# Attention output with plain fp32 values, two tiles side by side in the column halves of the matrix array

## The chip, the cores and the metric

The kernel runs on one core of a Trainium2 chip. The metric is device time in microseconds (us) for one launch; lower is better. The core has five engines that run their own instruction streams and wait for each other through semaphores: TensorE (PE; its weight loads are listed apart as PEld), VectorE (DVE), ScalarE (ACT), GpSimd (POOL) and SyncE (SP, which here only issues DMAs). Matrix products read SBUF and write PSUM; the other engines bring results from PSUM back to SBUF.

## The reference, cut to what matters

One mixer layer over 2048 latent tokens (a grid of 32 rows by 64 columns) and 256 context tokens, width 1024: RMSNorm with modulation, one input projection, two groups of heads, one output projection, gated residual, final RMSNorm. The group that the change touches is neighbourhood attention with 8 heads of 64:

```python
s_loc = einsum('bhrqd,bhrkd->bhrqk', qr, kg) * scale + bias      # window of 8 x 16 cells
s_ctx = einsum('bhrqd,bhcd->bhrqc', qr, k_ctx) * scale           # all 256 context keys
p = softmax(concatenate([where(mask, s_loc, -inf), s_ctx], -1))
o = einsum('bhrqk,bhrkd->bhrqd', p_loc, vg) + einsum('bhrqc,bhcd->bhrqd', p_ctx, v_ctx)
y_na = merge(o) * silu(na_g)
```

The other group is retention (a chunkwise recurrence). Everything is float32.

## The kernel before, in words

**Precision.** Most products are made from operands that are split into a rounded part (fp32r) and its remainder; three of the four cross products are summed in PSUM. A few products, the retention's and the modulation's (`ada_mm`, L296), use plain fp32 operands; each such matmul is recorded as two weight loads and two matmuls, one pass after the other.

**Stages.** First the projections (L343, L354, L656), whose results go to DRAM scratch tensors. The values are made by `u_v`: ACT copies the projected tile as rounded part, DVE subtracts for the remainder, and both 64-column pieces are stored side by side as 128 columns per head in `vB` (latent) and `vS` (context). The attention stage follows, then retention and the output projection.

**The attention stage.** A head's 2048 queries are cut into 16 tiles of 128 queries (8 rows by 16 columns, `dims`): index i over row bands, j over column bands. With 8 heads there are 128 tiles, and one step of the main loop (`for t in range(NT + 3)`) works on four of them at once, in a software pipeline written out by hand:

- `s_mm(t)`: scores of tile t into the PSUM tile `sS` (L1019, local keys and context keys, two halves of the split query each);
- `s_norm(t - 1)`: DVE reciprocal (L1038), POOL multiplies the probabilities (L1039);
- `s_min(t)`: DVE adds the bias and takes the row's maximum (L1028);
- `p_tr(t - 2)`: PE transposes 3 or 4 local groups of keys (L1046) and 2 context groups (L1048) into the PSUM tile `tr`; ACT copies them to `pt` as the rounded part (L1050);
- `s_exp(t)`: ACT exponential (L1033);
- `p_lo(t - 2)`: DVE subtracts the rounded part from `tr` for the remainder (L1056);
- `pv(t - 3)`: PE multiplies values by probabilities. The stationary operand holds 128 columns (rounded value, remainder), the moving one 256 (rounded probability, remainder), so that one matmul makes four partial products (L1067 local, L1069 context);
- every second step `combine`: ACT copies one partial product (L1090), DVE adds three of them (L1091, L1093), and for every fourth tile POOL multiplies by the gate (L1097).

Between these, `fill` issues pieces of the remaining projections, about two a step: six matmuls of 256 columns (L354) or three of 512 (L343). When such a unit ends, its own DVE, ACT or POOL work is issued at that place: for the rotary q projection three DVE operations (L382, L383, L384), for the rotary k projection four (L418, L419). All engines take their instructions in the written order. `load_v`, `load_gate`, `load_q` and `bias` issue their DMAs on SP, stores go through ACT's queue.

Of the kernel before, what the change touches and what calls it, by code (L numbers as in the profile page):

```python
# [18 lines left out]
P = 128  # L19
# [61 lines left out]
def hybrid_kernel(ctx: ExitStack, tc: tile.TileContext, a: dict, out: bass.AP):  # L81
# [5 lines left out]
    kS = [dram.tile([P, 2, LT], F32, name=f"kS{t}") for t in range(4)]  # L87
    vS = [dram.tile([LC, 4, P], F32, name=f"vS{t}") for t in range(2)]
    vB = [dram.tile([P, 8, 4, 4 * P], F32, name=f"vB{t}") for t in range(2)]
    gS = [dram.tile([P, L], F32, name=f"gS{t}") for t in range(4)]  # L90
# [297 lines left out]
    def u_v(w, c0, tp):  # L388
        pm = yield from tokform(w, tp)
        vt = op.tile([P, 4, 4, 64], F32R, name="o")  # L390
        pv = pm.rearrange("p (g e d) -> p g e d", e=2, d=64)
        nc.scalar.copy(vt[:, :, ::3, :], pv)
        nc.vector.tensor_tensor(vt[:, :, 1:3, :], pv, f(vt)[:, :, ::3, :], ALU.subtract)
        s, o = (c0 - 1024) // WG, f(vt).rearrange("p (t h) e d -> p t (h e d)", t=2)
# [584 lines left out]
    def load_head(h):  # L979
        k2 = kp.tile([P, LT], F32R, name="k2")  # L980
        for hl in range(2):
            nc.sync.dma_start(f(k2)[64 * hl:64 * hl + 64, :], kS[h // 2][64 * (h % 2):64 * (h % 2) + 64, hl, :])
        vc = kp.tile([P, 2, P], F32R, name="vc")
        nc.sync.dma_start(f(vc), vS[h // 4][:, h % 4, :].rearrange("(n p) d -> p n d", p=P))
        return dict(k2=k2, h=h, vc=vc, vt={}, q={})
# [8 lines left out]
    def load_v(hd, gs):  # L994
        for g in gs:
            vt, h = kp.tile([P, 4, P], F32R, name="vt", bufs=6), hd["h"]
            for e, n in ((0, P), (2, 96)):
                nc.sync.dma_start(f(vt)[:n, e:e + 2, :], vB[h // 4][:n, g, e:e + 2, (h % 4) * P:(h % 4 + 1) * P])
            hd["vt"][g] = vt
# [4 lines left out]

    heads, ys, tl_st = {}, {}, {}

# [34 lines left out]
    def p_tr(t):  # L1041
# [8 lines left out]
        nc.scalar.copy(pt[:, :ng_ + 2, 0, :], tr[:, :ng_ + 2, :])  # L1050
        T.update(pt=pt, ng=ng_)

    def p_lo(t):
        T = tl_st[t]
        pt, n = T["pt"], T["ng"] + 2
        nc.vector.tensor_tensor(pt[:, :n, 1, :], tr[:, :n, :], f(pt)[:, :n, 0, :], ALU.subtract)  # L1056

    def pv(t):
        h, i, j, kr0, kr, kc0, cw = dims(t)
        T, hd = tl_st[t], heads[h]  # L1060
        pt, ng_ = T["pt"], T["ng"]
        if t % 2 == 0:
            tl_st["po"] = psc.tile([P, 2, 2, P], F32, name="po")
        po = tl_st["po"]
        cn = 4 * cw
        for g in range(ng_):
            nc.tensor.matmul(po[:, t % 2, :, :], hd["vt"][kr0 // 4 + g][:cn, VORD.index(j), :], pt[:cn, g, :, :], start=(g == 0), stop=False)  # L1067
        for g in range(2):
            nc.tensor.matmul(po[:, t % 2, :, :], hd["vc"][:, g, :], pt[:, ng_ + g, :, :], start=False, stop=(g == 1))  # L1069
        del tl_st[t]  # L1070

# [5 lines left out]
    def load_gate(t):  # L1077
        h, i = dims(t)[:2]
        gts[t // 4] = ap_.tile([P, 512], F32, name="gt", bufs=2)
        nc.sync.dma_start(gts[t // 4][fin_(h)], gS[h // 2][fin_(h), i * 512:(i + 1) * 512])  # L1080

    def combine(t):
        h, i, j = dims(t)[:3]
        po, jp = tl_st["po"], j // 2
        fin, oth = fin_(h), fin_(h + 1)
        if jp == 0:
            ys[i] = ap_.tile([P, 512], F32, name="y2", bufs=2)
        y2 = ys[i]
        tmp = ap_.tile([P, 2, P], F32, name="cmb", bufs=1)
        nc.scalar.copy(tmp[fin], po[oth, :, 0, :])  # L1090
        nc.vector.tensor_tensor(tmp[fin], po[fin, :, 0, :], tmp[fin], ALU.add)  # L1091
        yv = y2[fin].rearrange("p (r w c) -> p w r c", r=8, w=4)[:, 2 * jp:2 * jp + 2]
        nc.vector.tensor_tensor(yv, po[fin, :, 1, :].rearrange("p j (r c) -> p j r c", r=8),  # L1093
                                tmp[fin].rearrange("p j (r c) -> p j r c", r=8), ALU.add)
        if jp == 1:
            gt = gts.pop(t // 4)
            nc.gpsimd.tensor_tensor(y2[fin], y2[fin], gt[fin], ALU.mult)  # L1097
            store(yS[i // 2][h // 2, fin, (i % 2) * 512:(i % 2) * 512 + 512], y2[fin], 2)

# [125 lines left out]
    for t in range(NT + 3):  # L1225
# [392 lines left out]
```

## Time and profile before

| | |
|---|---|
| time, median of 3 runs | 1346.33 us (1343.83 to 1348.54) |
| the profiled execution, its own time | 1343.91 us |
| its span in the trace | 1342.1 us |
| busy: PE, PEld, DVE, ACT, POOL | 96%, 86%, 62%, 45%, 43% |
| granted TensorE clock | 0.996 |

The span is what the trace covers of that execution; 1.8 us lie around it. Matmuls are pipelined: a row's duration includes the way through the array, so the time that a matmul costs in a stream is read from the distance between two starts. In rows of the timeline the first number is the start, the second the time until the last one of the row ends; "x4" counts the instructions in it. In a group's row stand busy time and the mean of one in ns, and behind the bar how long its engine stood idle just before, and what it waited for. `128*32` means 128 rows and 32 columns of the array.

### The profile page before, as it was taken

What the parts mean: (1) busy time and instruction counts of PE and PEld (TensorE: products, weight loads), DVE (VectorE), ACT (ScalarE), POOL (GpSimd) and SP (SyncE); (2) the same over time, 40 slices, a digit from 0 to 9 for tenths busy, and PEclk for the clock granted to TensorE, in tenths of its full rate; (3) what the DMA queues carried; (4) which work ended last, traced back from release to release, by engine and by line L of the source; (5) the groups of instructions that cost most, each with busy time, mean ns of one, the idle gap of its engine ahead of it and who ended that gap; (6) DMA issues with size and microseconds to landing.
All of it is one profiled execution on the core that took longest, in us unless ns stands there. A gap on an engine that the chain in (4) does not pass through costs nothing. (4 is left out here: it accounts for less than half of the span.)

```text
span 1342.1 us, 23118 instructions
## 1 busy us (share of the span) xinstructions
PE 1292.9 (96%) x8252; PEld 1148.2 (86%) x8252; DVE 831.2 (62%) x1442; ACT 602.5 (45%) x1252; POOL 574.9 (43%) x567
## 2 busy tenths in 40 slices
PE   5989999999999999999999999999999999999997
PEld 2677899887898889998999889889999788888886
DVE  4786365876676763477767777776654734444445
ACT  3454334243434334555565466556643244333432
POOL 3452102455115664454535365655523154544442
PEclk9999999999999999999999999999999999999999
DMA  9386797565867657967587887776547888445433
GB/s 362 142 282 235 267 321 207 188 219 185 320 181 230 217 176 244 256 205 196 155 219 211 231 221 210 188 183 197 157 158 255 283 288 269 156 157 173 165 128 123
DMA packets 172084, 287.24 MB, mean 214 GB/s; under 512 B 17345, under 2 KB 92225, under 8 KB 170690
## 3 DMA queue, kind: packets, MB, share of 16 engines
q1 hardware_dynamic: 139554, 228.35, 56.5%
q10 hardware_dynamic: 32416, 57.42, 11.9%
q8 instruction: 66, 1.08, 0.4%
q14 instruction: 48, 0.39, 0.1%
HBM read 194.48 MB, written 91.23 MB: 213 GB/s over the span
## 5 line engine op out<-in xcount | busy, mean ns | idle before, releaser
L354 PE MATMUL mm<-whi,hlo 128*128 128x256 f32 x832 | 228.1, 282 | 1.0 <-DMA hlo<-cS 1.0
L354 PE MATMUL mm<-whi,hhi 128*128 128x256 f32 x768 | 224.3, 292 | 0.0
L354 PE MATMUL mm<-wlo,hhi 128*128 128x256 f32 x768 | 216.8, 282 | 0.0
L1050 ACT CAST pt<-tr 128x640 fp32r<-128x640 f32 (+1 forms) x128 | 95.5, 746 | 160.3 <-PE tr L1048 157.7
L1056 DVE TENSOR_TENSOR pt<-tr,pt 128x640 fp32r<-128x640 f32 (+1 forms) x128 | 113.9, 890 | 78.3 <-ACT pt L1050 77.1
L354 PEld LDWEIGHTS mm<-whi,hlo 128*128 128x128 f32 x832 | 155.9, 190 | 1.4 <-DMA hlo<-cS 1.3
L1039 POOL TENSOR_SCALAR sp<-sp,stt 128x640 f32<-128x640 f32 (+2 forms) x128 | 103.2, 808 | 106.5 <-DVE stt L1038 77.8
L354 PEld LDWEIGHTS mm<-whi,hhi 128*128 128x128 f32 x768 | 146.1, 190 | 0.0
L354 PEld LDWEIGHTS mm<-wlo,hhi 128*128 128x128 f32 x768 | 145.7, 190 | 0.0
L610 POOL TENSOR_TENSOR whi<-st,whi 128x512 fp32r<-128x512 f32 x48 | 64.7, 1370 | 158.7 <-ACT whi L609 158.7
L1028 DVE CUSTOM_DVE_ANT_0 sp<-sS,nb 128x640 f32<-128x640 f32 (+2 forms) x128 | 105.6, 825 | 34.1 <-DMA nb<-in_rpb_t_dram 21.5
L1033 ACT ACTIVATE sp<-sp,stt 128x640 f32<-128x640 f32 (+2 forms) x128 | 107.4, 839 | 20.5 <-DVE stt L1028 19.3
L343 PE MATMUL mm<-hhi,whi 128*128 128x512 f32 x256 | 108.6, 424 | 0.5 <-ACT hhi L261 0.5
L343 PE MATMUL mm<-hlo,whi 128*128 128x512 f32 x256 | 102.0, 398 | 5.8 <-DVE hlo L282 2.4
L1019 PE MATMUL sS<-k,q 128*128 128x256 f32 (+3 forms) x512 | 99.1, 315 | 5.7 <-DVE stt L1028 5.5
L343 PE MATMUL mm<-hhi,wlo 128*128 128x512 f32 x256 | 101.7, 397 | 0.0
L1459 PE MATMUL mm<-wor,y 128*128 128x512 f32 x384 | 95.6, 398 | 1.7 <-DVE xt L1468 1.2
L656 PE MATMUL mm<-hhi,whi 128*128 128x512 f32 x336 | 96.8, 393 | 0.0
L1468 DVE TENSOR_TENSOR xt<-mm,xt 128x512 f32<-128x512 f32 x64 | 43.9, 687 | 82.5 <-PE mm L1459 82.5
L1019 PEld LDWEIGHTS sS<-k,q 128*128 128x128 f32 x512 | 82.7, 188 | 12.6 <-DVE stt L1028 8.8
L1459 PE MATMUL mm<-won,y 128*128 128x512 f32 x336 | 89.1, 403 | 0.0
L1459 PEld LDWEIGHTS mm<-wor,y 128*128 128x128 f32 x384 | 69.9, 188 | 18.0 <-issue 3.7
(253 smaller groups left out, 3018.3 us busy)
## 6 DMA issues: line engine op xcount, KB each, us to landing
st<-in_w_in_dram SPq DMA_DIRECT2D x64, 512.0 KB
q<-qS SPq DMA_DIRECT2D x64, 256.0 KB
hlo<-hS SPq DMA_DIRECT2D x20, 512.0 KB
k<-kS SPq DMA_DIRECT2D x16, 576.0 KB
kS<-o SPq DMA_DIRECT2D x16, 512.0 KB
vB<-o SPq DMA_DIRECT2D x64, 128.0 KB
qS<-o ACTq DMA_DIRECT2D x16, 512.0 KB
woS<-g ACTq DMA_DIRECT2D x32, 256.0 KB
```

The lines of the kernel that those rows point to most:

```text
L343: nc.tensor.matmul(pm[:, :n], ww[:, k, cs], h[:, k, :], start=(k == 0 and i == 0), stop=(k == KC - 1 and i == 2))
L354: nc.tensor.matmul(pm[:, t * WG:(t + 1) * WG], h[:, k, o:o + P], ww[:, k, :], start=(k == 0 and i == 0), stop=(k == KC - 1 and i == 2))
L610: nc.gpsimd.tensor_tensor(t[:, 1], r, f(t)[:, 0], ALU.subtract)
L656: nc.tensor.matmul(pm, ww[:, k, :], hh[:, k, :], start=(k == 0 and i == 0), stop=(k == KH - 1 and i == 2))
L1019: nc.tensor.matmul(o, hd["q"][i][:, hl, j * P:(j + 1) * P], k, start=(hl == 0), stop=(hl == 1))
L1028: nc.vector.tensor_tensor_reduce(T["sp"][:, :n], T["s"], nbz[big][:, o:o + n], -1.0, 3e38, ALU.add, ALU.min, T["st"][:, 0:1])
L1033: nc.scalar.activation(sp[:, :n], sp[:, :n], AF.Exp, bias=st[:, 0:1], scale=-1.0, accum_out=st[:, 1:2])
L1039: nc.gpsimd.tensor_scalar(sp[:, :n], sp[:, :n], st[:, 2:3], 0.0, ALU.mult, ALU.add)
L1050: nc.scalar.copy(pt[:, :ng_ + 2, 0, :], tr[:, :ng_ + 2, :])
L1056: nc.vector.tensor_tensor(pt[:, :n, 1, :], tr[:, :n, :], f(pt)[:, :n, 0, :], ALU.subtract)
L1459: nc.tensor.matmul(pm, yy[:, k, :], ww[:, k, sl], start=(k == 0 and i == 0), stop=(k == 3 and i == 2))
L1468: nc.vector.tensor_tensor(xts[t][:, sl], pm, xts[t][:, sl], ALU.add)
```

## The change

Values and probabilities stay plain fp32 in the product of scores and values. `u_v` only copies (ACT); a head's values have 64 columns in `vB`, `vS`, `vt` and `vc`. `p_lo` goes: ACT copies the local groups of `tr` to `pt`, and DVE (`p_ctx`, new) copies the two context groups. `pv` now takes two tiles, j and j + 1 of one row band: tile j's result goes to PSUM partitions 0 to 63, that of j + 1 to partitions 64 to 127, with a stationary operand of 64 columns and 128 moving columns, and the two tiles' matmuls alternate. `pv` is called in every second step. `combine` is called in every fourth step, and is two DVE multiplies of PSUM by the gate; ACT's copy, DVE's two additions and POOL's multiply go. The gate is loaded into both halves of the partitions, by two DMAs instead of one. `po` is half as large and allocated once for four tiles; `pt` is half as large and has four buffers instead of two.

```diff
     def u_v(w, c0, tp):
         pm = yield from tokform(w, tp)
-        vt = op.tile([P, 4, 4, 64], F32R, name="o")
-        pv = pm.rearrange("p (g e d) -> p g e d", e=2, d=64)
-        nc.scalar.copy(vt[:, :, ::3, :], pv)
-        nc.vector.tensor_tensor(vt[:, :, 1:3, :], pv, f(vt)[:, :, ::3, :], ALU.subtract)
+        o = op.tile([P, 2, 512], F32, name="o")[:, 0, :]
+        nc.scalar.copy(o, pm)
...
-        pt = ap_.tile([P, 6, 2, P], F32R, name="pt")
-        nc.scalar.copy(pt[:, :ng_ + 2, 0, :], tr[:, :ng_ + 2, :])
-        T.update(pt=pt, ng=ng_)
-
-    def p_lo(t):
-        T = tl_st[t]
-        pt, n = T["pt"], T["ng"] + 2
-        nc.vector.tensor_tensor(pt[:, :n, 1, :], tr[:, :n, :], f(pt)[:, :n, 0, :], ALU.subtract)
+        T.update(pt=ap_.tile([P, 6, P], F32, name="pt", bufs=4), ng=ng_)
+        nc.scalar.copy(T["pt"][:, :ng_, :], tr[:, :ng_, :])
+
+    def p_ctx(t):
+        pt, ng_ = tl_st[t]["pt"], tl_st[t]["ng"]
+        nc.vector.tensor_copy(pt[:, ng_:ng_ + 2, :], tr[:, ng_:ng_ + 2, :])
 
     def pv(t):
-        h, i, j, kr0, kr, kc0, cw = dims(t)
-        T, hd = tl_st[t], heads[h]
-        pt, ng_ = T["pt"], T["ng"]
-        if t % 2 == 0:
-            tl_st["po"] = psc.tile([P, 2, 2, P], F32, name="po")
-        po = tl_st["po"]
-        cn = 4 * cw
-        for g in range(ng_):
-            nc.tensor.matmul(po[:, t % 2, :, :], hd["vt"][kr0 // 4 + g][:cn, VORD.index(j), :], pt[:cn, g, :, :], start=(g == 0), stop=False)
-        for g in range(2):
-            nc.tensor.matmul(po[:, t % 2, :, :], hd["vc"][:, g, :], pt[:, ng_ + g, :, :], start=False, stop=(g == 1))
-        del tl_st[t]
+        h, i, j, kr0 = dims(t)[:4]
+        hd, pr = heads[h], [tl_st.pop(t + e) for e in range(2)]
+        if j == 0:
+            tl_st["po"] = psc.tile([P, 2, P], F32, name="po")
+        po, ng_ = tl_st["po"], pr[0]["ng"]
+        for g in range(ng_ + 2):
+            for e in range(2):
+                cn = 4 * CWIN[j + e][1] if g < ng_ else P
+                v = hd["vt"][kr0 // 4 + g][:cn, VORD.index(j + e), :] if g < ng_ else hd["vc"][:, g - ng_, :]
+                nc.tensor.matmul(po[64 * e:64 * e + 64, j // 2, :], v, pr[e]["pt"][:cn, g, :], start=(g == 0), stop=(g == ng_ + 1))
...
-        nc.sync.dma_start(gts[t // 4][fin_(h)], gS[h // 2][fin_(h), i * 512:(i + 1) * 512])
+        for e in range(2):
+            nc.sync.dma_start(gts[t // 4][64 * e:64 * e + 64], gS[h // 2][fin_(h), i * 512:(i + 1) * 512])
...
-        nc.scalar.copy(tmp[fin], po[oth, :, 0, :])
-        nc.vector.tensor_tensor(tmp[fin], po[fin, :, 0, :], tmp[fin], ALU.add)
...
-            nc.gpsimd.tensor_tensor(y2[fin], y2[fin], gt[fin], ALU.mult)
-            store(yS[i // 2][h // 2, fin, (i % 2) * 512:(i % 2) * 512 + 512], y2[fin], 2)
+        for e in range(2):
+            es = slice(64 * e, 64 * e + 64)
+            nc.vector.tensor_tensor(tok(y2[fin])[:, e], po[es].rearrange("p j (r c) -> p j r c", r=8), tok(gt[es])[:, e], ALU.mult)
+        store(yS[i // 2][h // 2, fin, (i % 2) * 512:(i % 2) * 512 + 512], y2[fin], 2)
...
         if 0 <= t - 2 < NT:
-            p_lo(t - 2)
+            p_ctx(t - 2)
         fill(part[1])
-        if 0 <= t - 3 < NT:
-            pv(t - 3)
-            if (t - 3) % 2 == 1:
+        if 0 <= t - 3 < NT and (t - 3) % 2 == 1:
+            pv(t - 4)
+            if (t - 3) % 4 == 3:
                 combine(t - 3)
```

The order in which PE takes its instructions changes. Before, in step 12 of the main loop, from the transposes to the next step's scores (`tr` are the transposes, `mm` a piece of fill, `po` scores times values, `sS` the next scores; a plain fp32 matmul is one row here and two recorded passes in a trace):

```order
L1046 MATMUL tr<-ident,sp 128x128 x4
L1048 MATMUL tr<-ident,sp 128x128 x2
L354 MATMUL mm<-whi,hhi 128x256
L354 MATMUL mm<-whi,hlo 128x256
L354 MATMUL mm<-wlo,hhi 128x256
L354 MATMUL mm<-whi,hhi 128x256
L354 MATMUL mm<-whi,hlo 128x256
L354 MATMUL mm<-wlo,hhi 128x256
L1067 MATMUL po<-pt,vt 128x256 x4
L1069 MATMUL po<-pt,vc 128x256 x2
L1019 MATMUL sS<-k_4588,q 128x384 x2
L1019 MATMUL sS<-k_4588,q 128x256 x2
```

Every step has these six matmuls of `po`. In the changed kernel the same place reads, in step 12:

```order
L1044 MATMUL tr<-ident,sp 128x128 x4
L1046 MATMUL tr<-ident,sp 128x128 x2
L354 MATMUL mm<-whi,hhi 128x256
L354 MATMUL mm<-whi,hlo 128x256
L354 MATMUL mm<-wlo,hhi 128x256
L354 MATMUL mm<-whi,hhi 128x256
L354 MATMUL mm<-whi,hlo 128x256
L354 MATMUL mm<-wlo,hhi 128x256
L1064 MATMUL po<-pt,vt 64x128 x8
L1064 MATMUL po<-pt,vc 64x128 x4
L1017 MATMUL sS<-k_4570,q 128x384 x2
L1017 MATMUL sS<-k_4570,q 128x256 x2
```

In step 13 of the changed kernel, from the scores to the next scores:

```order
L1044 MATMUL tr<-ident,sp 96x128 x4
L1046 MATMUL tr<-ident,sp 128x128 x2
L354 MATMUL mm<-whi,hhi 128x256
L354 MATMUL mm<-whi,hlo 128x256
L354 MATMUL mm<-wlo,hhi 128x256
L354 MATMUL mm<-whi,hhi 128x256
L354 MATMUL mm<-whi,hlo 128x256
L354 MATMUL mm<-wlo,hhi 128x256
L1017 MATMUL sS<-k_4570,q 128x384 x2
L1017 MATMUL sS<-k_4570,q 128x256 x2
```

Twelve matmuls of two tiles stand in one step, and none in the next: steps with even t hold them, steps with odd t do not.

On DVE, around step 59, where a rotary q unit ends at the first of the three fill places. Before (L1056 is `p_lo`, L1091 and L1093 `combine`, L1028 `s_min`, whose second row reads its maximum):

```order
L1056 TENSOR_TENSOR pt<-tr,pt 128x6x128
L1091 TENSOR_TENSOR cmb<-po,cmb 64x256
L1093 TENSOR_TENSOR y_7378<-po,cmb 64x2x8x16
L1038 RECIPROCAL stt<-stt 128x1
L382 TENSOR_TENSOR o<-mm,rot 64x512
L383 TENSOR_TENSOR o<-mm,rot 64x512
L384 TENSOR_TENSOR o<-mm,rot 128x512
L1028 ISA sp,stt<-sS,nb_4585 128x640
L1028 ISA stt 128x1
L1056 TENSOR_TENSOR pt<-tr,pt 128x6x128
```

In the changed kernel, at the same place (L1052 is `p_ctx`, L1084 the multiplies by the gate, L1026 `s_min`):

```order
L1052 COPY pt<-tr 128x256
L1084 TENSOR_TENSOR y_7338<-po,gt 64x2x8x16 x2
L1036 RECIPROCAL stt<-stt 128x1
L382 TENSOR_TENSOR o<-mm,rot 64x512
L383 TENSOR_TENSOR o<-mm,rot 64x512
L384 TENSOR_TENSOR o<-mm,rot 128x512
L1026 ISA sp,stt<-sS,nb_4567 128x640
L1026 ISA stt 128x1
L1052 COPY pt<-tr 128x256
```

The three rotary operations still stand ahead of `s_min`; the six-group subtraction is a two-group copy, and the two additions are two multiplies, which now come in every fourth step only.

More of the change, by code (lines that the diff above doesn't have):

```diff
@@ L87, in hybrid_kernel @@
     kS = [dram.tile([P, 2, LT], F32, name=f"kS{t}") for t in range(4)]
-    vS = [dram.tile([LC, 4, P], F32, name=f"vS{t}") for t in range(2)]
-    vB = [dram.tile([P, 8, 4, 4 * P], F32, name=f"vB{t}") for t in range(2)]
+    vS = [dram.tile([LC, 4, 64], F32, name=f"vS{t}") for t in range(2)]
+    vB = [dram.tile([P, 8, 4, WG], F32, name=f"vB{t}") for t in range(2)]
     gS = [dram.tile([P, L], F32, name=f"gS{t}") for t in range(4)]
@@ L982, in load_head @@
             nc.sync.dma_start(f(k2)[64 * hl:64 * hl + 64, :], kS[h // 2][64 * (h % 2):64 * (h % 2) + 64, hl, :])
-        vc = kp.tile([P, 2, P], F32R, name="vc")
-        nc.sync.dma_start(f(vc), vS[h // 4][:, h % 4, :].rearrange("(n p) d -> p n d", p=P))
+        vc = kp.tile([P, 2, 64], F32, name="vc")
+        nc.sync.dma_start(vc, vS[h // 4][:, h % 4, :].rearrange("(n p) d -> p n d", p=P))
         return dict(k2=k2, h=h, vc=vc, vt={}, q={})
```

24 lines of the change are left out of this document (8 added, 16 removed).

## The prediction

> **What bounds the kernel now.** I read the page's busy times first, then the busy times by stage, then what PE waited for in the stage that changes.
>
> ```profile
> PE 1292.9 (96%) x8252; PEld 1148.2 (86%) x8252; DVE 831.2 (62%) x1442; ACT 602.5 (45%) x1252; POOL 574.9 (43%) x567
> ```
>
> The table by stage has time, then busy us of PE, PEld, DVE, ACT and POOL, then the clock and the DMAs' share:
>
> ```profile
> 553.00:1003.00 450.00, 439.35 (x3297) 414.76 (x3296) 321.66 (x717) 259.28 (x537) 228.04 (x249) 1.00 0.72 197
> ```
>
> In the attention stage, 450 us long, PE is busy for 439 us at full clock, DVE for 322, and the DMAs have room. So the stage is PE's own work plus what PE waits. The weight loads' waits show it (us, times, longest):
>
> ```profile
> PEld sS L1019 <- DVE stt L1028: 8.1, 13, 1.6
> PEld tr L1046 <- POOL sp L1039: 7.4, 14, 1.6
> PEld po L1067 <- ACT pt L1050: 2.8, 3, 1.3
> ```
>
> They come to 18.3 us. An edit can help in two ways here: less work on PE, or less of these 18 us. What DVE, ACT or POOL save beyond that ends nothing earlier.
>
> **The change, part by part. PE's old work goes.** Groups of the stage, and one step's starts:
>
> ```profile
> L1067 PE MATMUL po<-pt,vt 128*128 128x256 f32 (+1 forms) x448 | 74.3, 282 | 1.8 <-ACT pt L1050 0.9 <-DVE y L1093 0.9
> L1069 PE MATMUL po<-pt,vc 128*128 128x256 f32 x256 | 51.4, 282 | 0.0
> 802.83 0.65 PE L1067 MATMUL po<-pt,vt 128*128 128x256 f32 x4
> 803.32 0.41 PE L1069 MATMUL po<-pt,vc 128*128 128x256 f32 x2
> 803.56 0.64 PE L1019 MATMUL sS<-k,q 128*128 128x512 f32 x2
> ```
>
> Six matmuls, and with them the way to the next scores, take 0.73 us, 0.12 each. 448 + 256 = 704 of them cost 704 x 0.12 = 84.5 us. They go.
>
> **PE's new work.** Plain fp32 with 128 moving columns is in the trace, in retention:
>
> ```profile
> 1207.25 0.38 PE L1369 MATMUL mm<-v,sd 128*128 128x128 f32 x2
> 1207.47 0.39 PE L1370 MATMUL mm<-sb,qs 128*128 128x128 f32 x2
> 1207.70 0.39 PE L1371 MATMUL mm<-sf,qs 128*128 128x128 f32 x2
> ```
>
> One such matmul is two passes, and the next starts 0.22 us later: 0.111 us a pass. Whether two matmuls in different columns of the array run side by side is shown by the only ones that do not use all 128 columns:
>
> ```profile
> 42.41 0.40 PE L343 MATMUL mm<-hlo,whi 128*128 128x512 f32 x1
> 42.64 0.40 PE L343 MATMUL mm<-hhi,wlo 128*128 128x512 f32 x1
> 42.97 1.06 PE L296 MATMUL mm<-hlo,silw 128*32 128x512 f32 x8
> 43.97 0.50 PE L343 MATMUL mm<-hhi,whi 128*128 128x512 f32 x1
> 44.31 0.40 PE L343 MATMUL mm<-hlo,whi 128*128 128x512 f32 x1
> ```
>
> Four matmuls of 512 columns, eight passes, in four groups of 32 columns. One after the other they would take 8 x 4 x 0.111 = 3.55 us; the next L343 starts 1.00 us after them. That is two passes, 0.89 us, and little more: the groups run side by side. I take the same for two halves of 64. A pair of tiles then needs, for 5.5 groups of keys on average (704 / 128), 11 pass times of 0.111, or 1.22 us; 64 pairs 78.1 us. Two loads of 64 columns stand behind two passes in place of one load of 128, so I allow 0.105 to 0.117 a pass: 74 to 82 us.
>
> **The price of leaving and entering the full width** is in the same rows. From the L343 at 42.64 to the second one after the block, at 44.31, are 1.67 us. Two ordinary distances (42.41 to 42.64) are 0.46, the two passes 0.89: 0.32 us are lost for each excursion, the array running empty before and after it, with a first weight load that nothing covers. Here the first loads have 64 columns in place of 32, so I take 0.34; 64 pairs make 64 excursions, 21.8 us (0.25 to 0.40 each: 16 to 26). New work is 78.1 + 21.8 = 99.9 us, 15.4 more than the old (bounds 74 + 16 - 84.5 = 5.5 and 82 + 26 - 84.5 = 23.5).
>
> **DVE, ACT and POOL.** The groups that go, and the row by which I price `p_ctx`:
>
> ```profile
> L1056 DVE TENSOR_TENSOR pt<-tr,pt 128x640 fp32r<-128x640 f32 (+1 forms) x128 | 113.9, 890 | 78.3 <-ACT pt L1050 77.1
> L1091 DVE TENSOR_TENSOR cmb<-po,cmb 64x256 f32<-64x256 f32 x64 | 27.0, 422 | 28.5 <-ACT cmb L1090 28.3
> L1093 DVE TENSOR_TENSOR y<-po,cmb 64x256 f32<-64x256 f32 x64 | 27.0, 422 | 2.2
> L1090 ACT COPY cmb<-po 64x256 f32<-64x256 f32 x64 | 23.5, 367 | 4.3 <-PE po L1069 2.7
> L1097 POOL TENSOR_TENSOR y<-y,gt 64x512 f32<-64x512 f32 x32 | 41.2, 1287 | 82.8 <-DVE stt L1038 41.4 <-DVE y L1093 29.4 <-issue 11.1
> L219 DVE COPY t<-rs 128x256 f32<-128x256 f32 x9 | 3.7, 411 | 7.4 <-POOL rs L214 7.4
> ```
>
> DVE loses 113.9 + 54.0 and gains 128 x 0.41 = 52.6 for `p_ctx` and 64 x 0.42 = 27 for the multiplies: 88 us less. It also no longer stands behind ACT (77 and 28 us idle). ACT loses 23.5 us and a third of its copies, POOL 41.2. None of it is on the path except through the 18.3 us of waits. In `u_v` 18 subtractions on DVE go, in a stage that PE fills too; I count nothing for them.
>
> **How much of the waits goes** depends on what they consist of. A long wait for the scores, DVE then PE:
>
> ```profile
> 749.82 0.43 DVE L1091 TENSOR_TENSOR cmb<-po,cmb 64x256 f32<-64x256 f32 x1 [0.36 <-ACT cmb L1090]
> 750.29 0.43 DVE L1093 TENSOR_TENSOR y<-po,cmb 64x256 f32<-64x256 f32 x1
> 750.75 0.16 DVE L1038 RECIPROCAL stt<-stt 128x1 f32<-128x1 f32 x1
> 750.94 0.69 DVE L382 TENSOR_TENSOR o<-mm,rot 64x512 f32<-64x512 f32 x1
> 752.96 0.81 DVE L1028 CUSTOM_DVE_ANT_0 sp<-sS,nb 128x640 f32<-128x640 f32 x1
> ...
> 748.88 0.75 PE L1019 MATMUL sS<-k,q 128*128 128x384 f32 x4
> 750.06 0.28 PE L354 MATMUL mm<-wlo,hhi 128*128 128x256 f32 x1
> 750.19 0.60 PE L1046 MATMUL tr<-ident,sp 128*128 128x128 f32 x4
> 751.55 0.64 PE L1067 MATMUL po<-pt,vt 96*128 96x256 f32 x4
> 752.03 0.40 PE L1069 MATMUL po<-pt,vc 128*128 128x256 f32 x2
> 753.83 0.77 PE L1019 MATMUL sS<-k,q 128*128 128x288 f32 x4 [1.41 <-DVE stt L1028]
> ```
>
> This is step 59, with a rotary unit that ends at the first fill place. Its three operations (2.0 us) stand ahead of `s_min`, and PE's next scores wait for `s_min`. In the changed kernel the 0.86 us of L1091 and L1093 are gone from ahead of them, but the unit's last matmul (750.06) ends no earlier, so `s_min` gains only some 0.5 us. PE, for its part, is at the scores 0.72 us sooner, because an odd step holds no `po` matmuls any more. The wait stays or grows: from 748.88 the minimum is ready after 4.9 - 0.5 = 4.4 us (752.96 + 0.81 less 748.88, less the gain), and PE is back after 3.4 - 0.7 = 2.7 (752.03 and two times 0.12). Read off the written order, eight odd steps have such a unit ahead of `s_min`, four rotary q (a wait of 1.7 us) and four rotary k. Of the latter's operations a row says 0.41 us each:
>
> ```profile
> L418 DVE TENSOR_TENSOR o<-mm,rot 128x256 f32<-128x256 f32 x24 | 9.9, 411 | 0.2 <-PE mm L354 0.2
> ```
>
> Four of them are at most 1.6 us, 0.4 less than the 2.0 of rotary q, and they partly end earlier; between none and 1.3 us of wait I take 0.6 each. Together 6.8 + 2.4 = 9.2 us. The even steps, which now last some 4.4 us, lose theirs. So the 8.1 us become about 9, moved into fewer steps. The waits on POOL keep the work that fills POOL when blocks are reloaded, and lose the gate multiply (1.29 us in every fourth step): 7.4 go to about 4. Those on `po` (2.8) go to 1, since a new `po` now has two steps of room. 18.3 become 9 + 4 + 1 = 14: minus 4 (bounds minus 8, if rotary k's waits and POOL's go too, and plus 2).
>
> **SP and the DMAs.** `load_gate` issues 32 more DMAs on SP, ahead of the loads of the next head. SP has room, since it mostly stands still for buffers:
>
> ```profile
> SPq L998 <- PE po L1067: 111.4, 27, 9.7
> ```
>
> These loads of values wait for the last `pv` of a row band, which is an odd tile and stays in the same step, so they start no later; their bytes halve. Zero.
>
> **Sum.** 1343.9 (profiled) + 15.4 - 4 = 1355.3 us. The median of the runs is 2.4 us above the profiled execution; on it, 1346.3 + 11.4 = 1357.7, say 1358. Own range 1346.3 + 5.5 - 8 = 1344 to 1346.3 + 23.5 + 2 = 1372; both ends at once are unlikely, so 1346 to 1369 is meant.
>
> **The rivals.** *The waits go* (the other side: not slower). If DVE's and POOL's relief ends all 18.3 us, the sum is 15.4 - 18.3 = -3: 1343. It decides at the odd steps: the minimum would have to be ready 2.7 us after the scores' start. For it speaks that DVE is freed of 88 us and of 105 us behind ACT; against it the step above. 0.10.
>
> *The excursion costs nothing* between matmuls of 256 and 128 columns: 15.4 - 21.8 - 4 = -10, 1336. Against it: the same 0.33 us stand between 42.64 and 42.97, and 0.34 between 43.97 and 44.31, where neighbours are 0.23 apart. 0.07.
>
> *The halves run one after the other.* One half may have 96 rows and the other 128, and no row of the trace has such a pair, nor halves of 64. Then each pair has 22 pass times: 78 us more, 1436. 0.06.
>
> *Weight loads are not covered.* In these rows all eight loads of the four column groups, those of the second pass included, start within 0.16 us while the first pass runs:
>
> ```profile
> 42.97 0.16 PEld L296 LDWEIGHTS mm<-hlo,silw 128*32 128x32 f32 x8 [0.37 <-issue]
> 43.97 0.19 PEld L343 LDWEIGHTS mm<-hhi,whi 128*128 128x128 f32 x1 [0.84 <-issue]
> ```
>
> If they had to wait for the passes here, each of 704 pass times would be longer by a load of 64 columns. A bare load of 128 costs 0.34 - 0.23 = 0.11 us (43.97 to 44.31), half of it 0.055: 39 us more, 1397. 0.04. The Trainium skill has a rule that says so: in "TensorE: Matmul & The Clock Gate", Part 3, under what overlaps and what doesn't, weight loads overlap running matmuls only where the row groups differ, and here both halves use the same rows. By that rule 1397; the trace speaks against it, with eight loads in 0.16 us.
>
> **How the numbers follow.** 0.73 are left for the forecast. A measurement of this kernel can tell about 0.3%, or 4 us, from no change: below 1342.3 is faster, above 1350.4 slower. Faster: 0.07 of the free excursion and 0.03 of the case in which the waits go, 0.10. Same: 0.07 of that case and 0.09 for the low end of the forecast, 0.16. Slower: 0.64 of the forecast, 0.06 and 0.04, 0.74. The range is 1342 to 1372: it leaves out the free excursion, a part of the case in which the waits go, and the two dear ones, 0.20.
>
> **What would show it.** Right: the `po` passes of a pair at 0.11 us from pass to pass, both halves starting within a few hundredths; about 0.3 us of extra distance around each block; the waits for L1026 some 8 us, all in odd steps; DVE's busy time near 740 us. Wrong: passes of a pair 0.22 apart (halves in turn), or 0.16 (loads uncovered); no extra distance at the blocks; PE's waits under 5 us or over 25.

## The result, and the profile after

| | before | after |
|---|---|---|
| median of 20 runs each | 1345.58 us (1342.81 to 1348.54) | 1347.88 us (1345.62 to 1351.79) |
| ratio, 95% interval | | 1.0019 [1.0011, 1.0026], +2.5 us |
| attention stage, first scores to last `po` matmul | 544.76 to 1001.44, 456.7 us | 549.98 to 1010.17, 460.2 us |
| from there to the end of the span | 340.7 us | 339.8 us |

The change costs 2.5 us, within the 0.3% that the prediction counts as no change; the forecast was +11.4. The profiled execution of after took 1351.79 us, 3.9 above its median: its attention stage starts 5.2 us later than that of before, and TensorE's granted clock averaged 0.94 in the first 130 us, against 0.97 before. That the clock alone makes the 5.2 us is not shown. So the two traces are compared by stretches, not by their ends.

The page's busy times of after, and its attention stage as a row of the table by stage (time, then PE, PEld, DVE, ACT, POOL, clock, DMA share):

```profile
PE 1307.4 (97%) x8956; PEld 1144.1 (85%) x8956; DVE 742.3 (55%) x1360; ACT 548.3 (41%) x1188; POOL 534.4 (40%) x535
553.00:1003.00 450.00, 445.61 (x3944) 403.03 (x3944) 243.00 (x655) 207.39 (x480) 191.44 (x222) 1.00 0.70 188
```

DVE is relieved as worked out (742 against "near 740"), in the stage from 321.66 to 243.00. PE is idle for 4.4 us of the 450 where it was 10.6. The changed kernel's groups in the stage:

```profile
L1064 PE MATMUL po<-pt,vt 96*64 96x128 f32 (+1 forms) x896 | 63.0, 280 | 0.0
L1064 PE MATMUL po<-pt,vc 128*64 128x128 f32 x512 | 38.9, 272 | 0.0
L1052 DVE COPY pt<-tr 128x256 f32<-128x256 f32 x128 | 54.3, 424 | 92.9 <-ACT pt L1048 92.8
L1084 DVE TENSOR_TENSOR y<-po,gt 64x256 f32<-64x256 f32 x64 | 27.0, 422 | 29.8 <-PE po L1064 27.6 <-DMA gt<-gS 1.2
```

One pair of tiles on PE, then its weight loads (start, time until the last one ends; x16 counts passes of both halves):

```profile
754.47 0.40 PE L343 MATMUL mm<-hhi,wlo 128*128 128x512 f32 x1
754.79 1.09 PE L1064 MATMUL po<-pt,vt 128*64 128x128 f32 x16
755.72 0.61 PE L1064 MATMUL po<-pt,vc 128*64 128x128 f32 x8
756.25 0.85 PE L1017 MATMUL sS<-k,q 128*128 128x384 f32 x4
```

```profile
754.79 0.85 PEld L1064 LDWEIGHTS po<-pt,vt 128*64 128x64 f32 x16 [0.36 <-issue]
755.61 0.47 PEld L1064 LDWEIGHTS po<-pt,vc 128*64 128x64 f32 x8
756.25 0.19 PEld L1017 LDWEIGHTS sS<-k,q 128*128 128x128 f32 x1 [0.17 <-issue]
```

24 passes, 12 for each half. If the halves took turns at 0.11 us, the block would last 2.6 us; from 754.79 to 756.25 are 1.46. So both halves run together, at 0.109 us a pass by the starts of single passes, and the weight loads run along with them. Around the block, starts are further apart than in a stream: 0.09 us ahead of it (754.47 to 754.79, less 0.23), 0.05 after its first pass, 0.09 behind it and, by the distance from there to the second matmul of the scores, 0.11 at the weight load of 756.25, which nothing covers. That is 0.34 to 0.35 an excursion.

What PE's weight loads waited for in the same 450 us:

```profile
PEld sS L1017 <- issue: 8.1, 47, 0.2
PEld po L1064 <- issue: 8.0, 22, 0.4
PEld sS L1017 <- DVE stt L1026: 6.4, 8, 1.4
...
PEld tr L1044 <- POOL sp L1037: 1.1, 2, 0.9
...
PEld sS L1017 <- DVE stt L1036: 0.3, 2, 0.2
```

The rows with "issue" are the excursions' own (47 and 22 times, 0.2 to 0.4 each). So is the last row: its two waits of 0.17 us stand where the array goes back to the full width, and the scores' first matmul starts 0.20 us after the last pass there, as it does where the row says "issue". Waits for another engine are 6.4 + 1.1 = 7.5 us at most, where they were 18.3. The forecast had 14.

### The profile page after: what moved, and what is told of

It reads as the page before. It is cut to its first block, busy times and chain, and to the rows that moved or that the text cites. A ratio compares the mean times of both kernels' runs of the same rounds, so it can differ in the third digit from the quotient of the medians.

```text
span 1350.0 us, 24122 instructions
## 1 busy us (share of the span) xinstructions
PE 1307.4 (97%) x8956; PEld 1144.1 (85%) x8956; DVE 742.3 (55%) x1360; ACT 548.3 (41%) x1188; POOL 534.4 (40%) x535
## 4 chain that ended last, share of the span: by engine, by line
PE 79%; DVE 8%; DMA 5%; issue 3%; POOL 3%; ACT 1%; SPq 0%; ACTq 0%; DVEq 0%; POOLq 0%
PE mm L354 21%; PE mm L1446 12%; PE mm L654 11%; PE mm L343 9%; PE po L1064 6%; PE sS L1017 6%; PE tr L1044 3%; PE tr L1046 2%; PE mm L1168 2%; DMA v<-rvS 1%; PE mm L1358 1%; PE mm L1357 1%; PE mm L1337 1%; PE mm L1356 1%; DMA ident<-in_ident_dram 1%
## 5 line engine op out<-in xcount | busy, mean ns | idle before, releaser
L354 PE MATMUL mm<-whi,hlo 128*128 128x256 f32 x832 | 228.1, 282 | 0.8 <-DMA hlo<-cS 0.8
L354 PE MATMUL mm<-whi,hhi 128*128 128x256 f32 x768 | 225.4, 294 | 0.0
L354 PE MATMUL mm<-wlo,hhi 128*128 128x256 f32 x768 | 216.9, 282 | 0.8 <-DVE wlo L327 0.8
L1048 ACT COPY pt<-tr 128x384 f32<-128x384 f32 (+1 forms) x128 | 68.2, 533 | 227.2 <-PE tr L1046 227.2
L354 PEld LDWEIGHTS mm<-whi,hlo 128*128 128x128 f32 x832 | 156.0, 190 | 1.2 <-DMA hlo<-cS 1.1
L354 PEld LDWEIGHTS mm<-whi,hhi 128*128 128x128 f32 x768 | 146.2, 190 | 1.8 <-issue 1.7
L354 PEld LDWEIGHTS mm<-wlo,hhi 128*128 128x128 f32 x768 | 145.8, 190 | 1.0 <-DVE wlo L327 1.0
L1026 DVE CUSTOM_DVE_ANT_0 sp<-sS,nb 128x640 f32<-128x640 f32 (+2 forms) x128 | 106.4, 831 | 69.2 <-PE sS L1017 63.3
L343 PE MATMUL mm<-hhi,whi 128*128 128x512 f32 x256 | 110.3, 431 | 0.6 <-ACT hhi L261 0.6
L343 PE MATMUL mm<-hlo,whi 128*128 128x512 f32 x256 | 103.6, 405 | 5.6 <-DVE hlo L282 2.2
L1017 PE MATMUL sS<-k,q 128*128 128x256 f32 (+3 forms) x512 | 103.1, 323 | 3.9 <-DVE stt L1026 3.9
L1052 DVE COPY pt<-tr 128x256 f32<-128x256 f32 x128 | 54.3, 424 | 92.9 <-ACT pt L1048 92.8
L343 PE MATMUL mm<-hhi,wlo 128*128 128x512 f32 x256 | 103.5, 404 | 0.0
```

The source lines that it names most:

```text
L343: nc.tensor.matmul(pm[:, :n], ww[:, k, cs], h[:, k, :], start=(k == 0 and i == 0), stop=(k == KC - 1 and i == 2))
L354: nc.tensor.matmul(pm[:, t * WG:(t + 1) * WG], h[:, k, o:o + P], ww[:, k, :], start=(k == 0 and i == 0), stop=(k == KC - 1 and i == 2))
L1017: nc.tensor.matmul(o, hd["q"][i][:, hl, j * P:(j + 1) * P], k, start=(hl == 0), stop=(hl == 1))
L1026: nc.vector.tensor_tensor_reduce(T["sp"][:, :n], T["s"], nbz[big][:, o:o + n], -1.0, 3e38, ALU.add, ALU.min, T["st"][:, 0:1])
L1048: nc.scalar.copy(T["pt"][:, :ng_, :], tr[:, :ng_, :])
L1052: nc.vector.tensor_copy(pt[:, ng_:ng_ + 2, :], tr[:, ng_:ng_ + 2, :])
```

## The experiments

The theory after this: PE's own work rose by the 15 us that were worked out, 22 of them excursions, and 10 to 12 us of PE's waits went because DVE, ACT and POOL were relieved. The rival cause: the waits went because PE's steps became longer and were paired, or because the transfers were halved. Each run is compared with runs of the kernel before on the same chip.

| run | median us | ratio to before, 95% interval |
|---|---|---|
| after | 1347.88 | 1.0019 [1.0011, 1.0026] |
| e1_sub_back | 1356.45 | 1.0075 [1.0053, 1.0097] |
| e2_old_pe_new_dve | 1332.42 | 0.9905 [0.9881, 0.9929] |
| e3_two_excursions | 1369.44 | 1.0177 [1.0152, 1.0202] |
| e4_four_tiles | 1340.98 | 0.9966 [0.9952, 0.9980] |
| e6_four_tiles_later | 1350.16 | 1.0049 [1.0030, 1.0068] |
| e7_four_tiles_act | 1341.10 | 0.9974 [0.9964, 0.9984] |
| e8_two_tiles_later | 1352.54 | 1.0060 [1.0045, 1.0075] |
| e9_four_later_act | 1348.07 | 1.0030 [1.0017, 1.0043] |
| e10_four_tiles_mult_after_min | 1342.37 | 0.9985 [0.9975, 0.9994] |
| e11_two_later_8_values | 1345.04 | 1.0005 [0.9995, 1.0015] |
| e12_mult_after_min | 1345.65 | 1.0008 [0.9997, 1.0018] |
| e13_four_later_8_values | 1347.42 | 1.0009 [0.9995, 1.0022] |

### The new PE work with the old DVE work: e1_sub_back

```diff
-        nc.scalar.copy(T["pt"][:, :ng_, :], tr[:, :ng_, :])
+        nc.scalar.copy(T["pt"][:, :ng_ + 2, :], tr[:, :ng_ + 2, :])
...
-        nc.vector.tensor_copy(pt[:, ng_:ng_ + 2, :], tr[:, ng_:ng_ + 2, :])
+        lo = ap_.tile([P, 6, P], F32, name="plo", bufs=1)
+        nc.vector.tensor_tensor(lo[:, :ng_ + 2, :], tr[:, :ng_ + 2, :], pt[:, :ng_ + 2, :], ALU.subtract)
```

> The kernel after, with the two relieved engines loaded again as before and nothing else changed: ScalarE copies all 8 (4 local and 2 context, or as many as the tile has) groups of probabilities out of PSUM, and VectorE does a full-width subtraction of PSUM and that copy into a scratch tile, in the place of its small copy. TensorE's instructions, the pairing of tiles and the transfers stay as in the kernel after. Theory (TensorE's own work rises by some 15 us, and some 11 us of its waits go because VectorE's step is shorter): the 704 subtractions hold the next minimum back again, the waits at the scores in the short steps come back, and the time is 6 to 11 us over the kernel after, 1354 to 1359 us. Rival (the waits went because the excursions and the pairing lengthened TensorE's steps, or because the transfers were halved): at most 2 us over the kernel after, up to 1350 us.

1356.45 us, 8.6 over after by the medians and 7.5 by the ratios. The weight loads' waits in 553 to 1003 us:

```profile
PEld sS L1017 <- DVE stt L1026: 8.1, 12, 1.4
...
PEld tr L1044 <- issue: 3.3, 13, 0.4
PEld sS L1017 <- DVE stt L1036: 3.3, 19, 0.2
PEld tr L1044 <- POOL sp L1037: 2.2, 4, 1.0
```

PE's instructions, the pairing and the transfers are those of after, so the rival's "at most 2 us" is out. The time is the theory's, but mostly not by the waits that it named. The minimum's waits rise from 6.4 to 8.1 us only, and the five long ones, in steps 15, 55, 59, 99 and 103, are those of after to 0.01 us. The row behind the reciprocal (L1036) is no new wait: these are exits of 0.17 us, which in after stood under "issue" (47 + 2 there, 25 + 19 here). Most of what is new stands at the transposes, in the row "issue" above all. In 18 of their 20 waits of 0.1 us and more, the transposes start 0.15 us after the end of the subtraction L1053, while POOL's multiply had ended 1.3 us earlier or more: the subtraction still reads `tr`, which the next transposes write.

### The old PE work with the new DVE work: e2_old_pe_new_dve

```diff
-        pt, n = T["pt"], T["ng"] + 2
-        nc.vector.tensor_tensor(pt[:, :n, 1, :], tr[:, :n, :], f(pt)[:, :n, 0, :], ALU.subtract)
+        pt, g = T["pt"], slice(T["ng"], T["ng"] + 2)
+        nc.vector.tensor_tensor(pt[:, g, 1, :], tr[:, g, :], f(pt)[:, g, 0, :], ALU.subtract)
...
-        nc.scalar.copy(tmp[fin], po[oth, :, 0, :])
-        nc.vector.tensor_tensor(tmp[fin], po[fin, :, 0, :], tmp[fin], ALU.add)
...
+        nc.vector.tensor_tensor(half(y2), po[fin, :, 0, :].rearrange("p j (r c) -> p j r c", r=8), half(gts[t // 4]), ALU.mult)
```

> The kernel before, with TensorE's instructions as they were, and VectorE's, ScalarE's and GpSimd's share cut about to that of the kernel after: the subtraction covers only the two context groups, and a pair's combination is one VectorE multiply by the gate from PSUM (the copy, the two additions and the GpSimd multiply are gone). It leaves out the remainder of the local probabilities (zeros stand for it) and one of the two partial products of each pair. Theory: TensorE's work stays, its waits at the scores and the transposes fall by some 11 us of the 18, so the time is 1333 to 1337 us. Rival (the waits went by the longer steps of TensorE or by the transfers): 1343 to 1346 us, as the kernel before.

1332.42 us, 12.8 under before by the ratio, the lowest of all; PE's instructions and the transfers are those of before. ScalarE still copies all groups here. The waits of the same stretch, 3.4 us in all where before had 18.3:

```profile
PEld sS L1022 <- DVE stt L1031: 1.3, 3, 0.5
PEld tr L1049 <- POOL sp L1042: 1.0, 2, 0.6
PEld po L1070 <- DVE y L1093: 0.7, 2, 0.4
PEld tr L1049 <- POOL wlo L327: 0.4, 1, 0.4
```

So the two halves of the change come apart: the relief alone is worth 12.8 us, and the new PE work beside about the same relief costs 15.3 (1.0019 against 0.9905). These 15.3 are not PE's work alone, since after waits 7.5 us and e2 3.4. With e1, the relief is shown to be the main cause. One small part belongs to the rival: in steps 26, 30, 70 and 74, where before waited 1.3 us, the minimum of after is ready no more than 0.05 us earlier, and PE comes to the next scores some 0.8 us later, because these even steps hold the passes of a pair. The share of the combination and of POOL's gate multiply was not run by itself.

### The price of an excursion: e3_two_excursions

```diff
-        for g in range(ng_ + 2):
+        for g in (range(ng_, ng_ + 2) if last else range(ng_)):
...
+        if 0 <= t - 3 < NT and (t - 3) % 2 == 1:
+            pv(t - 4, False)
         fill(part[1])
         if 0 <= t - 3 < NT and (t - 3) % 2 == 1:
-            pv(t - 4)
+            pv(t - 4, True)
```

> The kernel after, with each pair's passes split: the local groups of both tiles ahead of the filling work of that step, the two context groups behind it, so that TensorE goes into 64-column passes and back 128 times instead of 64. The same passes, the same work on the other engines. Theory (an excursion costs 0.345 us and lies on the path): 64 more of them give +22 us, 1368 to 1372 us. Rival (most of that time is given back out of the waits, because a longer step lets VectorE catch up): +5 to +12 us, 1353 to 1360 us.

1369.44 us, 21.6 over after by the medians, 21.3 by the ratios: 0.33 to 0.34 us for each of 64 more. One pair on PE, with the work between its two parts:

```profile
759.48 1.09 PE L1064 MATMUL po<-pt,vt 128*64 128x128 f32 x16
760.50 0.50 PE L343 MATMUL mm<-hhi,whi 128*128 128x512 f32 x1
760.84 0.40 PE L343 MATMUL mm<-hlo,whi 128*128 128x512 f32 x1
761.07 0.39 PE L343 MATMUL mm<-hhi,wlo 128*128 128x512 f32 x1
761.39 0.66 PE L1064 MATMUL po<-pt,vc 128*64 128x128 f32 x8
761.98 0.44 PE L1017 MATMUL sS<-k,q 128*128 128x384 f32 x1
```

The entry (761.07 to 761.39) and the exit (760.50 to 760.84 is the uncovered load) show the same prices as in after. The rival is out: PE's waits for other engines fell only from 7.5 to some 6 us, so nearly all of the excursions' time lies on the path.

### Half as many excursions: e4_four_tiles

```diff
         if 0 <= t - 3 < NT and (t - 3) % 2 == 1:
-            pv(t - 4)
             if (t - 3) % 4 == 3:
+                pv(t - 6)
+                pv(t - 4)
                 combine(t - 3)
```

(and six buffers of `pt`).

> The kernel after, with the passes of two pairs of tiles in one block every fourth step (6 buffers of probabilities instead of 4), so that TensorE goes into 64-column passes and back 32 times instead of 64. Theory: 32 excursions of 0.345 us fewer, -11 us, 1335 to 1340 us, faster than both kernels. Rival: the steps without passes become shorter than VectorE's work of a step, and the new waits there eat 4 us or more of it: 1341 to 1346 us.

1340.98 us: 7 us under after and 0.34% under before, faster than both kernels. That is between the two readings, at the rival's end: 32 excursions are worth 11 us, and 4 of these were eaten. The waits show where:

```profile
PEld sS L1017 <- DVE stt L1026: 8.8, 11, 1.4
...
PEld tr L1044 <- POOL sp L1037: 2.1, 3, 0.9
```

They are 10.9 where after had 7.5; three of four steps are now short ones.

### Trying to move the last waits: e6, e7, e8, e9

In after 4.2 us of the remaining waits, by the distances between starts, stand in steps 15, 55, 59, 99 and 103, in e4 the same 4.2 of 8.4. e6 moves the block of four tiles one step later, so that these steps hold it; e8 does so with the pairs of after; e7 gives ScalarE the whole copy; e9 is e6 with e7.

```diff
-        if 0 <= t - 3 < NT and (t - 3) % 2 == 1:
-            pv(t - 4)
-            if (t - 3) % 4 == 3:
-                combine(t - 3)
+        if 0 <= t - 4 < NT and (t - 4) % 2 == 1:
+            pv(t - 5)
+            if (t - 4) % 4 == 3:
+                combine(t - 4)
```

(e8; e6 has `(t - 4) % 4 == 3` with `pv(t - 7)`, `pv(t - 5)`; both one step more and one more buffer of `pt`.)

> The kernel with four tiles in one block (32 excursions, 1340.98 us), with the block and its combination one step later: in the fourth step of each four (15, 55, 59, 99, 103 among them, where 4.2 us of TensorE's remaining waits for the scores' minimum stand) in place of the third; 7 buffers of probabilities in place of 6. Theory (the waits left over stand where a rotary unit's last operations meet a step without passes, so they go when the passes come to that step): -3 to -4 us against four tiles a step earlier, 1337 to 1338 us. Rival (any short step that holds such a unit waits, and the combination's two multiplies now hold up the minimum of the first step of each four): no gain or a loss, 1340 to 1344 us.

> The kernel with four tiles in one block (1340.98 us), where ScalarE copies all the probabilities out of PSUM and VectorE's 128 copies of the context groups (0.41 us each) are gone. Theory (VectorE's queue ahead of the minimum is what TensorE still waits for, 9.2 us at the scores): some ten waits shorter by 0.3 to 0.4 us each, -3 to -4 us, 1337 to 1338 us. Rival (what is left is the unit's own last three operations, and the copy did not stand ahead of them): within 1 us, 1340 to 1342 us.

> The kernel after, with each pair's passes and combination one step later, in the odd steps in place of the even ones (5 buffers of probabilities in place of 4); 64 excursions as in the kernel after. In the kernel after all but one of the waits for the scores stand in odd steps, 0.5 to 1.3 us each, at the rotary units. Theory: the odd steps become 1.6 us longer and lose these waits, the even ones hold fewer such units: -3 to -4 us against the kernel after, 1344 to 1345 us. Rival (the waits move into the even steps, which are now short): within 1 us of the kernel after, 1347 to 1349 us.

> Four tiles in one block, one step later, and ScalarE copying all the probabilities (the two last edits together). Theory: if both edits take away different waits, -6 to -8 us against four tiles in one block, 1333 to 1335 us, the fastest of these kernels. Rival (both take away the same waits, or neither any): 1337 to 1341 us.

By the medians e6 lost 9.2 us against e4 and e8 4.7 against after (11.2 and 5.5 by the ratios): the theory missed, and by more than the rivals said. e7 gained nothing (its rival: 128 copies fewer on DVE, and the waits behind the minimum still 8.1 us). e9 lost 7.1 against e4 (8.6 by the ratios) and missed both of its readings. In e8 the waits for the minimum did fall, from 6.4 to 3.0 us. But one new wait stands at the transposes. The rows of e8, ACT, DVE, then PE:

```profile
914.03 0.41 ACT L325 CAST whi<-st 128x256 fp32r<-128x256 f32 x1 [7.74 <-DMA st<-in_w_in_dram]
914.34 0.58 ACT L1048 COPY pt<-tr 128x512 f32<-128x512 f32 x1
914.95 0.42 DVE L1052 COPY pt<-tr 128x256 f32<-128x256 f32 x1 [5.60 <-ACT pt L1048]
```

```profile
911.28 0.28 PE L354 MATMUL mm<-wlo,hhi 128*128 128x256 f32 x1
915.52 1.09 PE L1044 MATMUL tr<-ident,sp 128*128 128x128 f32 x4 [3.96 <-DVE pt L1052]
```

and SP's waits, e8 then after:

```profile
SPq L996 <- PE po L1064: 139.5, 27, 10.4
```

```profile
SPq L996 <- PE po L1064: 105.9, 28, 9.2
```

SP issues the loads of the values (L996) in order with all others. They wait for the `po` passes that free a buffer; a step later, SP stands 139.5 us behind them instead of 105.9, and a weight load (`st`) behind them comes late. ACT waits 7.7 us for it, and ACT's copy of `tr`, next in its order, starts at 914.34 only; DVE's copy follows, and the next transposes, which write `tr`, start 0.15 us after it. In e6 a similar wait was 4.2 us, another behind a late load of the query 2.0.

### The queue as the cause: e11, and two more orders, e12, e10, e13

e11 is e8 with eight buffers of values instead of six; e12 is after, e10 is e4, with the combination's multiplies behind the next step's minimum; e13 is e6 with both.

```diff
-            vt, h = kp.tile([P, 4, 64], F32, name="vt", bufs=6), hd["h"]
+            vt, h = kp.tile([P, 4, 64], F32, name="vt", bufs=8), hd["h"]
```

```diff
         if 0 <= t - 2 < NT:
             p_ctx(t - 2)
+        if 0 <= t - 4 < NT and (t - 4) % 4 == 3:
+            combine(t - 4)
```

> The kernel with two tiles a step later (1352.54 us), with 8 buffers of values in place of 6. In its trace TensorE stands 4.1 us once (911 to 915 us) behind a weight split on GpSimd whose load was late in SyncE's queue, behind loads of values that wait for the passes; after it TensorE runs at a granted clock of 0.50 for 5 us. Theory (the later passes release the values' buffers later, and everything queued behind them on SyncE comes late): with 8 buffers these loads hardly wait, the single wait and the slow spell go, -5 to -7 us, 1346 to 1348 us. Rival (the load is late because of the DMAs' load there, whatever the queue): at most -2 us, 1350.5 to 1353 us.

1345.04 us, 7.4 under e8 by the ratios, a little more than the theory's 5 to 7. SP now waits 6.5 us at L996, and the wait of 4.1 us is gone:

```profile
SPq L996 <- PE po L1064: 6.5, 6, 1.4
```

The queue was the cause: SP issues the late weight load at 901.14 instead of 904.83. Its second half lands 11.4 us after its issue here and 10.1 in e8, with the DMA engines' share near 1.0 in both, so the full DMA engines are a condition of the wait, but not what changed. With it gone the later pairs are 2 to 3 us under after, close to what e8 was to gain; after itself with eight buffers was not run, so the two edits' shares are not apart.

> The kernel after, with nothing changed but that the combination's two multiplies stand behind the next step's minimum on VectorE instead of ahead of it. Theory: of the 5.0 us that TensorE still stands at the scores in the odd steps, 2 to 4 go, 1344 to 1346 us. Rival: within 1 us of the kernel after, 1347 to 1349 us.

> The kernel with four tiles in one block (1340.98 us), with the combination's two multiplies put behind the next step's minimum on VectorE instead of ahead of it. In its trace these multiplies (0.87 us) stand first in VectorE's queue in steps 15, 55, 59, 99 and 103, ahead of a rotary unit's operations and of the minimum for which TensorE waits 0.6 to 1.3 us. Theory (what VectorE has queued ahead of a minimum in a short step sets the wait): five waits shorter by 0.4 to 0.9 us each, -2 to -4 us, 1337 to 1339 us. Rival (the unit's own operations are released so late that the minimum gains nothing): within 1 us, 1340 to 1342 us.

> Four tiles in one block one step later (1350.16 us), with 8 buffers of values and the multiplies behind the next step's minimum. In the trace of the former, 6.4 us are two single waits on late loads with a slow spell behind one of them, and ten waits of 0.6 to 1.5 us stand in the first step of each four, where the multiplies come. Theory: the late loads' 8 to 9 us go and some 4 us of the waits behind the multiplies, 1336 to 1340 us. Rival (the waits of the short steps stay, only the loads' go): 1341 to 1344 us.

e12: 1.5 us under after by the ratios, 2.2 by the medians; the two intervals overlap, so this is a likely gain and no more. Its waits for the minimum fell from 6.4 to 1.8 us, all of its waits for another engine, without the exits' 0.2 us each, from 7.5 to 4.6. e10, the same edit on e4, gained nothing (1.4 us over e4 by the medians, 2.6 by the ratios): in step 59 the minimum is now ready 1.8 us after the scores' start where e4 needed 4.0, but the multiplies stand at the end of that step and delay the next, which in e4 is a short one too. After steps 8, 48 and 52 PE now waits 0.9 to 1.1 us, and the sum behind the minimum went from 8.8 to 10.7. e13 missed both readings: 1347.42, 2.7 under e6 by the medians and 5.4 by the ratios. The short steps' waits stayed, and so did 2.7 us behind the late load: ACT has its tile 4.5 us earlier than in e6 (914.21 against 918.73), but PE is at that place some 3 us earlier too.

## Why the prediction was wrong, point by point

**PE's old and new work: right, within some 1.5 us.** 11 pass times of 0.11 a pair and 0.34 an excursion gave +15.4. Passes measured 0.109 apart and e3's 0.34 an excursion make it 704 x 0.109 + 64 x 0.34 - 84.5 = +14.0. The stage of after is 17.9 us longer than that of e2 (460.2 against 442.3), and 4.1 of these are waits: 13.8. The rivals "the excursion costs nothing" and "the halves run one after the other" are out. So is "weight loads are not covered", and with it, for two column halves on the same rows, the rule of the Trainium skill ("TensorE: Matmul & The Clock Gate", Part 3, what overlaps and what doesn't) that loads overlap only where row groups differ: passes stand 0.109 us apart with a load each of 0.137.

**The waits: this step failed.** It said of step 59 that "the unit's last matmul (750.06) ends no earlier, so `s_min` gains only some 0.5 us", let this step stand for the odd steps, and so kept 9 + 4 + 1 = 14 us. Measured are 6.4 + 1.1 = 7.5: the term was -4 and is -10.8. Of the difference 2.8 us are the minimum's, 2.9 POOL's and 1.0 those on `po`. Step 59 in after, DVE then PE:

```profile
756.37 0.87 DVE L1084 TENSOR_TENSOR y<-po,gt 64x256 f32<-64x256 f32 x2 [1.12 <-PE po L1064]
757.28 0.16 DVE L1036 RECIPROCAL stt<-stt 128x1 f32<-128x1 f32 x1
757.47 0.69 DVE L382 TENSOR_TENSOR o<-mm,rot 64x512 f32<-64x512 f32 x1
...
759.48 0.81 DVE L1026 CUSTOM_DVE_ANT_0 sp<-sS,nb 128x640 f32<-128x640 f32 x1
```

```profile
757.55 0.28 PE L354 MATMUL mm<-wlo,hhi 128*128 128x256 f32 x1
...
758.92 0.28 PE L354 MATMUL mm<-wlo,hhi 128*128 128x256 f32 x1
760.36 0.77 PE L1017 MATMUL sS<-k,q 128*128 128x288 f32 x4 [1.16 <-DVE stt L1026]
```

The rotary operation L382 starts at 757.47, ahead of the last matmul of that fill place (757.55). So that matmul belongs to the next unit, and at 750.06 it did too: the unit's own matmuls had ended in an earlier place, and L382 had waited for nothing but its turn on DVE. The kernel says so as well, since a rotary q unit's products are made by L343 and 750.06 is a matmul of L354. A group's row of before says so, and I had not read it this way: the idle time ahead of its 12 executions is 0.4 us in all.

```profile
L382 DVE TENSOR_TENSOR o<-mm,rot 64x512 f32<-64x512 f32 x12 | 8.3, 694 | 0.4
```

What DVE's turn had waited for is in the rows ahead of it, in step 55 of before:

```profile
733.16 0.96 DVE L1056 TENSOR_TENSOR pt<-tr,pt 128x768 fp32r<-128x768 f32 x1 [1.10 <-ACT pt L1050]
734.48 0.43 DVE L1091 TENSOR_TENSOR cmb<-po,cmb 64x256 f32<-64x256 f32 x1 [0.36 <-ACT cmb L1090]
...
737.62 0.81 DVE L1028 CUSTOM_DVE_ANT_0 sp<-sS,nb 128x640 f32<-128x640 f32 x1
```

Subtraction and combination both stood behind ACT, and everything behind them on DVE came late. In these steps it was the combination that counted. The prediction had its 0.86 us "gone from ahead" of the unit, but the two multiplies by the gate (0.87) stand in the same place in steps 55 and 59. What went is their wait for ACT's copy L1090: in step 59 they start 0.12 us after the scores' start, where L1091 started at 0.94. In e1, with the subtraction back, it is 0.11 (757.28 against 757.17). In step 59 the minimum is ready 4.04 us after the scores' start (756.25 to 760.29) instead of 4.89, where I had 4.4, and PE is back after 2.8, where I had 2.7: the wait is 1.2 by its row, not 1.7. In step 55 the minimum came 1.07 us earlier (4.31 to 3.24 after the scores' start). I had counted four such units at 1.7 us and four at 0.6, 9.2 in all; the row of after says 8 waits and 6.4 us. Letting step 59 stand for the others was the larger error: the weight loads wait 1.37 us there, but 0.95, 1.05 and 0.67 in the other odd steps with rotary q (55, 99, 103), 4.0 in all instead of 6.8. Of the four with rotary k only step 15 waits, 1.05 us instead of 2.4 in all.

**POOL's waits** were put down to the work that fills POOL and to the gate multiply, and 4 us of 7.4 kept; 1.1 are left. The longest of before, in step 84, POOL then PE:

```profile
838.59 1.30 POOL L1097 TENSOR_TENSOR y<-y,gt 64x512 f32<-64x512 f32 x1
839.86 0.81 POOL L1039 TENSOR_SCALAR sp<-sp,stt 128x640 f32<-128x640 f32 x1
```

```profile
840.72 0.55 PE L1046 MATMUL tr<-ident,sp 128*128 128x128 f32 x3 [1.18 <-POOL sp L1039]
```

In six of the nine such waits of before (steps 20, 32, 64, 72, 84 and 127) the gate multiply stands directly ahead of the probabilities' multiply on POOL, as here. In after, e1 and e2, which have no gate multiply on POOL, a wait of 0.1 us or more for POOL's multiply of the probabilities is left in steps 31 and 86 alone. So the gate multiply held more of these waits than I gave it; the steps' new lengths may have a part in it. **The waits on `po`** went altogether (2.8 to none; I kept 1).

**SP and the DMAs: right, for the order as written.** The loads start no later, and e8 shows what the sentence was worth: one step later costs a wait of 4.1 us and a slow spell behind it.

**The rival that the waits go** came closest: 10.8 of the 18.3 us, not all. Of its two reasons, "freed of 105 us behind ACT" holds for the combination alone (28 us, which now wait for PE instead): the row of L1052 above still has 92.8 us behind ACT, where the subtraction had 77.

**Sum.** With the forecast's +15.4 for PE's work, 1343.9 + 15.4 - 10.8 = 1348.5 on the profiled execution of before, +4.6; with the measured +14.0 it is +3.2. The stage grew by 3.5 and the time behind it shrank by 0.9, together +2.6, the +2.5 of the runs.

## What to carry to other kernels

Before an operation is called late because of its producer, read the idle time ahead of its own group: near zero means that it waits for its turn in its engine's queue, and then everything removed ahead of it counts, the engine's own waits included. Take each step's own numbers, and do not let the longest stand for the others. Where a wait has no releaser in the rows, look for an engine that still reads the tile to be written. Where matmuls with few columns stand among full ones, price the way in and out of the narrow shape separately (0.34 us here) and gather them into fewer blocks; but a block that comes later frees its buffers later, and every load behind them in the same queue pays. Work moved out of one short step into the next short one only moves the wait.

## What the runs showed of the hardware

Two matmuls in the two 64-column halves start 7 ns apart on average, 11 at most, and run side by side also where one has 96 rows and the other 128. And an idle PE comes back slow. e8 around its wait, by stretches (the third number from the end is the granted clock):

```profile
911.00:915.50 4.50, 0.56 (x5) 0.37 (x4) 0.55 (x2) 1.47 (x3) 0.73 (x1) 0.81 1.05 315
915.50:917.00 1.50, 1.48 (x7) 1.50 (x8) 1.41 (x4) 1.14 (x5) 0.89 (x2) 0.50 1.00 223
917.00:919.00 2.00, 2.00 (x10) 1.81 (x9) 0.80 (x4) 1.93 (x5) 2.00 (x4) 0.50 0.82 175
919.00:921.00 2.00, 2.00 (x13) 2.00 (x12) 0.96 (x2) 0.07 (x1) 2.00 (x4) 0.59 0.75 262
```

After 4.1 us without work, five us at half clock follow: by an estimate from these two numbers (4.1 + half of 5.1) the wait cost some 6.6 us, close to the 7.4 that e11 won back. The Trainium skill has a rule for this in "TensorE: Matmul & The Clock Gate", Part 1: about 3.4 us without work bring half clock, and about 3.4 us of work full clock again. Neither is sharp here. In e8 the last matmul ends at 911.56, and a clock of 0.81 over the 4.50 us from 911.00 puts the fall at 913.8, after 2.2 us without work; full clock came back after 5.1 us of work, from 915.52 to 920.6. In e6 the wait was 4.2 us, and 3.3 us of work brought full clock back (920.2 to 923.5). In e13 a wait of only 2.7 us was followed by a spell at 0.50 too, while 2.0 us in e6 were not.
